# Block 2's projections in 512-wide matmuls, and bias tables copied by another queue

## The chip, the cores and the metric

One NeuronCore of one Trainium2 chip runs the whole program. The time is device microseconds of one execution, from launch to end. The engines are TensorE (PE in the profile, its weight loads PEld), VectorE (DVE), ScalarE (ACT), GpSimd (POOL) and SyncE (SP). They run side by side, each through its own queue of instructions in order, and wait for each other on semaphores.

## What is computed

Two transformer blocks on 256 tokens of width 1024, in float32. Block 1 has a gated convolution and recurrent mixer, cross-attention to a memory, and a mixture of 16 experts whose router picks a group and two experts in it. Block 2 has two layers over the tokens and 256 context tokens. In each layer one projection of the normalised input feeds three kinds of attention and their gates:

```
(na_q, na_k, na_v, cq, ckv, k_rope, dq, dk, dv, z, gm) = split(h @ w_in_l)
q, k = rms_norm(per head) * g ; rotary turn on some
o_na   = neighbourhood attention with a bias from na_rpb (8 heads of 64)
o_mla  = attention with low-rank q and k, v (8 heads of 96, w_uq, w_ukv)
o_diff = softmax(q0 k0) - lam * softmax(q1 k1), times v (4 heads)
y = sum over the three: sigmoid(gm_i) * ((o_i * silu(z_i)) @ w_br_i)
x = x + gate * (y @ w_out)
```

## The kernel before

Every large product is made of three: an operand is split into a rounded high part and the rest (`hi`, `lo`, type fp32r), and hi·hi + hi·lo + lo·hi are summed in PSUM. Weights arrive by SyncE's queue in units of 128 x 1024 numbers (512 KB, `_wdma`, L458), ScalarE makes the high part `wh`, VectorE the low part `wl` (`splitter`), and TensorE reads both. The small tiles all bear the name `t`, PSUM banks the name `p`, so the profile shows them so; nearly every operation is recorded by a helper (L369 matmul, L374 transpose, L382 ScalarE, L392 and its neighbours VectorE), so a group is known by its tiles. Names stand as out<-in, the moving operand first and the stationary one behind it.

There are two kinds of product. In `gemm_w` and `gemm_f` the weights are stationary and the tokens move (`p<-t,wh`). In `gemm_x`, `gemm_m` and `gemm_t` 128 tokens are stationary and the weights move (`p<-wh,t`, `p<-wl,t`). `gemm_t` (L683) serves Block 2: keys, values and queries of the neighbourhood and differential attention (`keys`, `queries`), the keys and values of the low-rank attention (`w_ukv_2` in `mla_half`), and the last projection `w_out_2` (`out`). It goes over 256 columns of weights at a time; a PSUM bank of 512 columns holds both halves (m = 0, 1) of one stream's 256 tokens side by side. A stream is the tokens (0) or the context (1); `both` asks for two.

What follows a product is its evacuation, spawned when its last matmul is out. For keys and queries that is `ev_qk`: ScalarE squares the bank, VectorE reduces it to a sum per head, `rsqrt` takes the root in ten small VectorE instructions (one root for both column halves, by `sums` and `roots`), VectorE multiplies the bank by it into a tile and frees the bank, a rotary turn follows for some, and `heads_T` transposes on TensorE and writes the heads by `put`. Values go through `ev_vals`, low-rank keys through `ev_kv`.

The program is written by a planner inside the kernel. Each piece of work is a generator (a fiber) with a priority and a time; `run` takes the fiber that TensorE, by the planner's own costs, could start first, and every instruction is put into its engine's queue when its fiber runs. PSUM has eight banks (`palloc`): products take at most six at a time, attention's scores and transposes four, its outputs three. A request for several banks waits until all are free. The order in which weight units are loaded is what the pass before asked for: a first pass without an order, then `PASSES` = 2 passes with the order of the one before, and the last is the program that runs.

For the neighbourhood attention, `prepare` (L921) writes for both layers a table of the bias in DRAM (`toep`), by sixteen copies from DRAM to DRAM of 448 rows of 64 numbers, issued on ScalarE's queue at L953; `TOEP` = 3000 ns of the planner's time lie between them. `attend` loads biases from it on GpSimd's queue (L2223). `GR` = 4 says that `out` goes over four column groups together for the first stream.

Of the kernel before, what the change touches and what calls it, by code (L numbers as in the profile page):

```python
# [13 lines left out]
AF = mybir.ActivationFunctionType  # L14
# [40 lines left out]
PASSES = 2  # L55
# [85 lines left out]
class Core:  # L141
# [15 lines left out]
    MEMT, TOEP, CRIT = 40000, 3000, -4  # L157
# [5 lines left out]
    GR, GP = 4, 0.5  # L163
# [519 lines left out]
    def gemm_t(self, name, lead, K, c0, c1, hi, lo, streams, evac, cw=256, base=0, kev=None, group=1):  # L683


        kt = K // 128
        evs = []
        for g in range(c0, c1, group * cw):
            pss = []
            for _ in range(group):  # L690
                ps = yield from self.palloc("pg", len(streams))
                pss.append(ps if len(streams) > 1 else [ps])
            for u in range(0, kt, 4):
                u1 = min(kt, u + 4)
                for i, ps in enumerate(pss):
                    c = g + i * cw
                    w = yield from self.wget(name, lead, u, u1, c, c + cw)
                    for p, s in zip(ps, streams):
                        for m in range(2):
                            o = p[:, m * cw:m * cw + cw]  # L700
                            t0 = T * (1 - s) + m * 128 - base
                            ts = slice(t0, t0 + 128)
                            for k in range(u, u1):
                                if kev:
                                    yield from self.wait(kev[k])
                                self.mm(o, hi.k(k)[:, ts], w.hi[:, k - u], m == 0 and k == 0, False)
                                self.mm(o, hi.k(k)[:, ts], w.lo[:, k - u], False, False)
                                self.mm(o, lo.k(k)[:, ts], w.hi[:, k - u], False, m == 1 and k == kt - 1)
                        if p is not ps[-1]:
                            yield  # L710
                    self.wput(w)
                    if u1 == kt:
# [208 lines left out]
    def prepare(self):  # L921
# [858 lines left out]
    def layer(self, l, hi, lo, C, ready, half=None):  # L1780
# [52 lines left out]
        def heads_T(raw, np_, nb, dst, d0, gain):  # L1833

            for j0 in range(0, nb, 2):
                jn = min(2, nb - j0)
                ps = yield from self.palloc("pa")
                pv = ps.rearrange("p (j t) -> p j t", j=2)
                for j in range(jn):
                    for m in range(2):  # L1840
                        self.tr(pv[:np_, j, m * 128:m * 128 + 128], raw(m, j0 + j))
                yield
                put(dst, slice(d0 + j0, d0 + j0 + jn), np_, slice(0, T), pv[:np_, :jn], gain)
                self.free(ps)
                yield
# [21 lines left out]
        def ev_qk(streams, gcol, dst, tab):  # L1867

            ns = len(streams)
            sh = yield from sums(2, ns * 8)  # L1870

            def evac(i, pss):
                ss = sh["ss"][:, i * ns * 8:(i + 1) * ns * 8].rearrange("p (m h) -> p m h", h=4)
# [9 lines left out]
                rv = r.rearrange("p (m h) -> p m h", h=4)  # L1883
                raws = []
                for a in range(ns):
                    rw = yield from self.alloc("S", [128, 2, 4, 64])
                    self.tt(rw, pv[a], rv[:, 2 * a:2 * a + 2][:, :, :, None].to_broadcast([128, 2, 4, 64]))
                    self.free(pss[a])
                    raws.append(rw)
                drop(sh)  # L1890
                yield
                for a, s in enumerate(streams):
                    rw = raws[a]
                    turn = tab is not None and s == 0
                    if turn:
                        yield from rope(rw, tabs[tab], 4, 64)
                    yield from heads_T(lambda m, j: rw[:, m, 2 * j:2 * j + 2].rearrange("p h d -> p (h d)"), 128, 2,
                                       dst[s], 2 * i, 1.0 if turn else gcol)
# [3 lines left out]
        def ev_vals(streams, v):  # L1902
            def evac(i, pss):
                for a, s in enumerate(streams):
                    self.act(v[s].kk(0, 2)[:, :, i * 256:i * 256 + 256], pss[a].rearrange("p (m c) -> p m c", m=2))
                    self.free(pss[a])
                    yield
            return evac

        def keys(ck, cv, gk, rot, streams):  # L1910
# [4 lines left out]
            ev = yield from ev_qk(streams, self.colv(gk, l), k, gk if rot else None)  # L1915
# [3 lines left out]
            evs += yield from self.gemm_t(W, (l,), D, cv, cv + 512, hi, lo, streams, ev_vals(streams, v))  # L1919
            return k, v, evs  # L1920

        def queries(cq, gq, rot, streams):
# [3 lines left out]
            ev = yield from ev_qk(streams, self.colv(gq, l), q, gq if rot else None)  # L1926
# [71 lines left out]
        def mla_half(i, lt):  # L1998
# [8 lines left out]
            shk = yield from sums(2, 8)  # L2007
            shq = yield from sums(2, 4 * ns)

            def ev_kv(c, pss):  # L2010
                ss = shk["ss"][:, c * 8:c * 8 + 8].rearrange("p (m h) -> p m h", h=2)
                t0 = self.cur.t
                pv = [p.rearrange("p (m h d) -> p m h d", m=2, h=2) for p in pss]
                sq = yield from self.alloc("S", [128, 4, 2, 64])
                for m in range(4):
                    p = pv[m // 2][:, m % 2]
                    r = st[:, 1, m:m + 1]
                    self.act(sq[:, m], p[:, :, 0:64], AF.Square, scale=r, after=t0)
                    self.act(v[1 - m // 2][:, m % 2].rearrange("p (h d) -> p h d", h=4)[:, 2 * c:2 * c + 2], p[:, :, 64:128], scale=r,
                             after=t0)  # L2020
                self.red(ss, sq)
                self.free(sq)
                self.tt(ss, ss, st[:, 2][:, :, None].to_broadcast([128, 4, 2]), OP.add)
                yield
                r = yield from roots(shk, c, 1.0 / 96)
                rv = r.rearrange("p (m h) -> p m h", h=2)
                rr = yield from self.alloc("T", [128, 4, 2])
                self.tt(rr, rv, st[:, 1][:, :, None].to_broadcast([128, 4, 2]))
                raws = []
                for a in range(2):  # L2030
                    rw = yield from self.alloc("S", [128, 2, 2, 96])
                    m2 = slice(2 * a, 2 * a + 2)
                    self.tt(rw[:, :, :, 0:64], pv[a][:, :, :, 0:64], rr[:, m2][:, :, :, None].to_broadcast([128, 2, 2, 64]))
# [706 lines left out]
```

## Time and profile before

| what | us |
|---|---|
| median of three runs | 1623.51 (1622.63 to 1624.02) |
| the profiled execution | 1620.66 |
| its span, first to last instruction | 1618.9 |
| TensorE busy in the span | 1560.7 |
| VectorE busy | 978.6 |
| ScalarE busy | 753.3 |
| GpSimd busy | 41.6 |

Busy is the union of an engine's instructions in the span. Matmuls overlap in the records, so the pace of a run of matmuls is read from their starts. The share of full clock that TensorE was granted stands in the windows as PEclk. In brackets behind a row of a timeline stands how long the engine had idled before it and what ended that; "issue" is idling for which the profile shows no releaser.

### The profile page before, as it was taken

To read this page: it belongs to the slowest core of one execution; us is meant where nothing else is said; L and a number is where in the kernel's file an instruction comes from. 1 tells how busy PE (TensorE), PEld (TensorE's weight loads), DVE (VectorE), ACT (ScalarE), POOL (GpSimd) and SP (SyncE) were. 2 spreads that over 40 slices of the span, in tenths; PEclk is the share of its full clock that TensorE was granted. 3 is DMA by queue.
4 is the path that set the end of the run, shared out by engine and by line. 5 is a ranking of instruction groups with operands and counts; after the bars stand their busy time and mean duration, and the time that the engine had idled before them with its cause. 6 is when DMAs were issued, how large, how long until landed. Compare 5 with 4: busy or idle time off the path is not lost.

```text
span 1618.9 us, 28924 instructions
## 1 busy us (share of the span) xinstructions
PE 1560.7 (96%) x11642; PEld 1319.7 (82%) x11642; DVE 978.6 (60%) x2035; ACT 753.3 (47%) x1357; POOL 41.6 (3%) x75
## 2 busy tenths in 40 slices
PE   6999999799999999999999999999989989999898
PEld 5898899653565558998888777889989989989898
DVE  5877457613232239778855555655866766867765
ACT  4524455333322127757743444553445464645552
POOL 0000000000000001011000000000100100000000
PEclk9999999899999999999999999999999999999999
DMA  9666556869999994665333444424655414333531
GB/s 342 230 215 222 182 182 194 283 249 383 372 381 336 378 377 151 182 175 118 92 110 110 145 133 149 137 74 157 206 156 156 119 53 144 112 102 106 157 110 62
DMA packets 233176, 305.31 MB, mean 189 GB/s; under 512 B 17184, under 2 KB 160288, under 8 KB 233040
## 3 DMA queue, kind: packets, MB, share of 16 engines
q1 hardware_dynamic: 222608, 293.11, 55.9%
q0 software_dynamic: 2576, 7.77, 1.6%
q10 hardware_dynamic: 7856, 2.56, 0.8%
q8 instruction: 93, 1.52, 0.4%
q14 instruction: 43, 0.35, 0.1%
HBM read 302.34 MB, written 2.90 MB: 189 GB/s over the span
## 4 chain that ended last, share of the span: by engine, by line
PE 61%; DVE 4%; ACT 2%; DMA 1%; issue 1%; DVEq 0%; ACTq 0%
PE p L369 56%; PE p L374 4%; ACT t L382 1%; DVE t L392 1%; DVE t L404 1%; DVE wl L392 1%; DMA w<-in_w_in_dram 1%; ACT wh L382 0%; DVE t L397 0%; DVE t L413 0%; DVE t L411 0%; DVE t L399 0%; DVE t L406 0%; DVE X L392 0%; ACT X L382 0%
## 5 line engine op out<-in xcount | busy, mean ns | idle before, releaser
L369 PE MATMUL p<-t,wh 128*128 128x256 f32 (+1 forms) x2640 | 562.6, 310 | 0.6 <-DVE t L392 0.6
L369 PE MATMUL p<-wh,t 128*128 128x256 f32 (+2 forms) x2248 | 466.2, 302 | 7.4 <-DVE t L392 5.7
L392 DVE TENSOR_TENSOR wl<-w,wh 128x1024 fp32r<-128x1024 f32 (+2 forms) x318 | 372.7, 1189 | 161.5 <-ACT wh L382 159.9
L369 PEld LDWEIGHTS p<-t,wh 128*128 128x128 f32 x2640 | 424.8, 190 | 35.0 <-issue 10.5
L369 PE MATMUL p<-t,wl 128*128 128x256 f32 (+1 forms) x1312 | 399.8, 305 | 4.0 <-DVE wl L392 4.0
L382 ACT ACTIVATE t<-p 128x512 f32<-128x512 f32 (+5 forms) x381 | 192.5, 528 | 443.9 <-PE p L369 335.3
L369 PEld LDWEIGHTS p<-wh,t 128*128 128x128 f32 x2248 | 367.0, 193 | 31.3 <-issue 8.8
L382 ACT ACTIVATE wh<-w 128x1024 fp32r<-128x1024 f32 (+2 forms) x318 | 319.4, 1032 | 52.1 <-issue 18.7
L369 PE MATMUL p<-wl,t 128*128 128x256 f32 (+2 forms) x1124 | 335.9, 299 | 0.9 <-DVE wl L392 0.9
L369 PEld LDWEIGHTS p<-t,wl 128*128 128x128 f32 x1312 | 250.1, 191 | 15.6 <-DVE wl L392 4.8
L369 PE MATMUL p<-t,t 128*64 128x128 f32 (+8 forms) x1824 | 220.4, 309 | 2.7 <-ACT t L382 1.6
L369 PEld LDWEIGHTS p<-wl,t 128*128 128x128 f32 x1124 | 216.6, 193 | 6.8 <-DVE wl L392 2.1
L369 PEld LDWEIGHTS p<-t,t 128*64 128x64 f32 (+3 forms) x1824 | 176.5, 171 | 38.7 <-issue 17.3
L369 PE MATMUL p<-w,t 128*64 128x512 f32 x768 | 174.0, 597 | 0.3 <-PEq L1641 0.3
L382 ACT ACTIVATE t<-p,t 128x512 f32<-128x512 f32 (+3 forms) x232 | 120.1, 559 | 115.6 <-PE p L369 75.2
L374 PE MATMUL p<-csts,t 128*128 128x128 f32 (+1 forms) x848 | 120.5, 282 | 24.4 <-ACT t L382 9.0
L374 PEld LDWEIGHTS p<-csts,t 128*128 128x128 f32 (+1 forms) x848 | 98.2, 143 | 41.9 <-issue 16.1
L369 PEld LDWEIGHTS p<-w,t 128*64 128x64 f32 x768 | 52.1, 136 | 95.0 <-issue 87.8
L392 DVE TENSOR_TENSOR t<-t,t 128x512 f32<-128x512 f32 (+9 forms) x254 | 108.8, 461 | 13.3 <-ACT t L382 10.4
L382 ACT ACTIVATE t<-p,cols 128x256 fp32r<-128x256 f32 (+4 forms) x91 | 49.9, 604 | 118.9 <-PE p L374 83.7
L404 DVE SCALAR_TENSOR_TENSOR t<-t,p 128x512 f32<-128x512 f32 x70 | 47.6, 683 | 84.4 <-ACT t L382 45.4
L411 DVE TENSOR_REDUCE t<-p 128x1 f32<-128x512 f32 (+1 forms) x124 | 84.8, 684 | 21.4 <-PE p L369 20.2
(95 smaller groups left out, 678.3 us busy)
## 6 DMA issues: line engine op xcount, KB each, us to landing
w<-in_w_in_dram SPq DMA_DIRECT2D x206, 512.0 KB, 4.3
w<-in_w_gate_dram SPq DMA_DIRECT2D x64, 512.0 KB, 8.6
w<-in_w_up_dram SPq DMA_DIRECT2D x64, 512.0 KB, 10.2
w<-in_w_down_dram SPq DMA_DIRECT2D x64, 512.0 KB, 10.3
w<-in_w_ada_dram SPq DMA_DIRECT2D x48, 512.0 KB, 3.7
w<-in_w_out_dram SPq DMA_DIRECT2D x32, 512.0 KB, 4.6
w<-in_w_br_dram SPq DMA_DIRECT2D x28, 512.0 KB, 3.4
w<-in_w_kv_dram SPq DMA_DIRECT2D x16, 512.0 KB, 4.8
```

The costliest lines, as they stand in the source:

```text
L369: self.nc.tensor.matmul(out, lhsT, rhs, start=start, stop=stop)
L374: self.nc.tensor.transpose(out, in_, self.ident[:k, :k])
L382: self.nc.scalar.activation(out, in_, func, bias=bias, scale=scale, **kw)
L392: self._e(eng, self._n(out), False, after).tensor_tensor(out, a, b, op=op)
L404: e.scalar_tensor_tensor(out, a, s, b, op0=op0, op1=op1)
L411: e.tensor_reduce(out, a, axis=AX, op=op, negate=True)
```

## The change

- `gemm_t` takes 512 columns at a time (units of 2 x 512 rows and columns in place of 4 x 256; 128 tokens now fill a bank of their own), so it asks for two banks for each stream. With `each`, every 128 tokens are evacuated as soon as their last matmul is out; values and `out` use that.
- `ev_qk`, `ev_kv`, `ev_vals`, `out` and `heads_T` follow that layout: one evacuation for 512 columns with its own root, transposes of four blocks of one half of the tokens. The turn is made for each half over 8 heads.
- `GR` is 2 in place of 4 (of twice the width). The output leaves as 128 tokens x 512 columns.
- The sixteen table copies are issued on GpSimd's queue, and `TOEP` is 20000.
- `PASSES` is 4, and the last pass takes, of the orders of the three before it, the one with the earliest planned end.

```diff
-PASSES = 2
+PASSES = 4
-    MEMT, TOEP, CRIT = 40000, 3000, -4
+    MEMT, TOEP, CRIT = 40000, 20000, -4
-    GR, GP = 4, 0.5
+    GR, GP = 2, 0.5
...
-    def gemm_t(self, name, lead, K, c0, c1, hi, lo, streams, evac, cw=256, base=0, kev=None, group=1):
+    def gemm_t(self, name, lead, K, c0, c1, hi, lo, streams, evac, cw=512, base=0, kev=None, group=1, each=False):
         kt = K // 128
+        ku = 1024 // cw
         evs = []
+        tiles = [T * (1 - s) + m * 128 - base for s in streams for m in range(2)]
         for g in range(c0, c1, group * cw):
             pss = []
             for _ in range(group):
-                ps = yield from self.palloc("pg", len(streams))
-                pss.append(ps if len(streams) > 1 else [ps])
-            for u in range(0, kt, 4):
-                u1 = min(kt, u + 4)
+                ps = yield from self.palloc("pg", len(tiles))
+                pss.append(ps)
+            for u in range(0, kt, ku):
+                u1 = min(kt, u + ku)
                 for i, ps in enumerate(pss):
                     c = g + i * cw
                     w = yield from self.wget(name, lead, u, u1, c, c + cw)
...
+                    for a, (p, t0) in enumerate(zip(ps, tiles)):
+                        ts = slice(t0, t0 + 128)
+                        for k in range(u, u1):
+                            if kev:
+                                yield from self.wait(kev[k])
+                            self.mm(p[:, :cw], hi.k(k)[:, ts], w.hi[:, k - u], k == 0, False)
+                            self.mm(p[:, :cw], hi.k(k)[:, ts], w.lo[:, k - u], False, False)
+                            self.mm(p[:, :cw], lo.k(k)[:, ts], w.hi[:, k - u], False, k == kt - 1)
+                        if u1 == kt and each:
+                            evs.append(self.spawn(evac((c - c0) // cw, a, p), prio=self.cur.prio - self.EVAC,
+                                                  name=f"evt {name} {c}"))
+                        if a % 2 and a < len(tiles) - 1:
                             yield
...
-                nc.scalar.dma_start(
+                nc.gpsimd.dma_start(
                     d[:, h].rearrange("c (r k) -> r c k", r=7),
...
+            n = 2 * len(streams)
+
+            def evac(_, pss):
+                ss = yield from self.alloc("T", [128, n, 8])
                 t0 = self.cur.t
-                pv = [p.rearrange("p (m h d) -> p m h d", m=2, h=4) for p in pss]
-                for a in range(ns):
-                    sq = yield from self.alloc("S", [128, 2, 4, 64])
+                pv = [p.rearrange("p (h d) -> p h d", h=8) for p in pss]
+                for a in range(n):
+                    sq = yield from self.alloc("S", [128, 8, 64])
                     self.act(sq, pv[a], AF.Square, after=t0)
-                    self.red(ss[:, 2 * a:2 * a + 2], sq)
+                    self.red(ss[:, a], sq)
                     self.free(sq)
                 yield
-                r = yield from roots(sh, i, 1.0 / 64)
+                r = yield from self.rsqrt(ss.rearrange("p a h -> p (a h)"), 1.0 / 64, n * 8)
...
+                for a in range(n):
+                    rw = yield from self.alloc("S", [128, 8, 64])
+                    self.tt(rw, pv[a], rv[:, a][:, :, None].to_broadcast([128, 8, 64]))
                     self.free(pss[a])
                     raws.append(rw)
...
-            evs += yield from self.gemm_t(W, (l,), D, cv, cv + 512, hi, lo, streams, ev_vals(streams, v))
+            evs += yield from self.gemm_t(W, (l,), D, cv, cv + 512, hi, lo, streams, ev_vals(streams, v), each=True)
...
+            def evac(i, m, ps):
+                c = slice(i * 512, i * 512 + 512)
+                tmp = yield from self.alloc("S", [128, 512])
+                self.tt(tmp, ps, g[:, c])
+                self.free(ps)
+                self.tt(res[m][:, c], tmp, res[m][:, c], OP.add)
                 self.free(tmp)
...
+    if order is None:
+        _passes.clear()
+    elif len(_passes) == PASSES - 1:
+        order = min(_passes, key=lambda x: x[0])[1]
     core = Core(tc.nc, tc, ctx, ins, out, order)
     core.program()
+    if order is not None:
+        _passes.append((max(core.E[e] for e in ("pe", "act", "dve")), order))
```

## Rows read from the trace of the kernel before

**Rows 1.** The page's first part: busy us, share of the span, instructions.

```profile
PE 1560.7 (96%) x11642; PEld 1319.7 (82%) x11642; DVE 978.6 (60%) x2035; ACT 753.3 (47%) x1357; POOL 41.6 (3%) x75
```

**Rows 2.** Groups by form on TensorE: shapes, count | busy us, mean ns | idle before.

```profile
L369 PE MATMUL p<-wh,t 128*128 128x256 f32 x1920 | 362.9, 287 | 6.0 <-DVE t L392 5.7 <-ACT t L382 0.2
...
L369 PE MATMUL p<-wl,t 128*128 128x256 f32 x960 | 273.8, 285 | 0.6 <-DVE wl L392 0.6
```

**Rows 3.** Timeline of TensorE at 1600 us: start us, us, instruction, count.

```profile
1600.11 0.40 PE L369 MATMUL p<-wh,t 128*128 128x256 f32 x2
...
1600.47 0.40 PE L369 MATMUL p<-wh,t 128*128 128x256 f32 x2
```

**Rows 4.** Timeline of TensorE at 146 us, `gemm_x`.

```profile
146.26 0.62 PE L369 MATMUL p<-wh,t 128*128 128x512 f32 x2
...
146.94 0.62 PE L369 MATMUL p<-wh,t 128*128 128x512 f32 x2
```

**Rows 5.** Timeline of all engines, 295 to 307 us; ACTq is ScalarE's queue.

```profile
295.88 0.28 PE L369 MATMUL p<-t,wrl 128*20 128x256 f32 x1
...
296.57 8.57 ACTq L953 DMA_DIRECT2D toep<-in_na_rpb_dram  x3
...
305.19 1.06 ACT L382 ACTIVATE wh<-w 128x1024 fp32r<-128x1024 f32 x1 [10.19 <-issue]
306.16 0.45 ACT L382 ACTIVATE t<-p,cols 20x256 f32<-20x256 f32 x1
...
306.66 0.40 PE L374 MATMUL p<-csts,t 20*128 20x20 f32 x2 [7.62 <-ACT t L382]
```

**Rows 6.** Windows: us, busy us (instructions) by engine, PEclk, DMA share, GB/s.

```profile
230.00:240.00 10.00, 10.00 (x52) 8.51 (x51) 5.38 (x10) 5.91 (x12) 0.00 (x0) 1.00 0.46 138
300.00:310.00 10.00, 3.34 (x14) 3.01 (x15) 3.06 (x6) 2.84 (x4) 0.00 (x0) 0.62 0.91 215
310.00:320.00 10.00, 8.59 (x62) 8.38 (x60) 7.74 (x33) 3.39 (x6) 0.00 (x0) 0.86 0.62 212
350.00:360.00 10.00, 10.00 (x65) 5.93 (x62) 0.65 (x2) 4.86 (x14) 0.00 (x0) 1.00 1.05 387
1135.00:1147.00 12.00, 12.00 (x102) 12.00 (x102) 8.43 (x9) 8.22 (x9) 0.00 (x0) 1.00 1.06 345
```

**Rows 7.** The copies' line: ns min/median/max of an issue, first and last start.

```profile
L953 ACTq DMA_DIRECT2D toep<-in_na_rpb_dram x16: 755/1059/4437, 244.0 to 301.9; - x16
```

**Rows 8.** Waits of SyncE's queue: us in total, times, longest us.

```profile
SPq L458 <- DMA toep<-in_na_rpb_dram: 24.4, 5, 8.1
```

**Rows 9.** Timeline of GpSimd.

```profile
522.83 0.55 POOL L1445 DMA_DIRECT2D t<-in_final_norm_dram  x1 [297.92 <-PE p L369]
...
700.02 2.46 POOL L2223 DMA_DIRECT2D t<-toep  x4 [72.63 <-PE p L369]
709.54 2.38 POOL L2223 DMA_DIRECT2D t<-toep  x4 [7.06 <-DVE wl L392]
```

**Rows 10.** Timeline of VectorE and TensorE, 1308 to 1311 us.

```profile
1308.61 2.48 DVE L392 TENSOR_TENSOR t<-p,t 128x512 f32<-128x512 f32 x4
1309.36 0.55 PE L369 MATMUL p<-wh,t 128*128 128x256 f32 x1 [5.11 <-DVE t L392]
...
1309.92 0.63 PE L369 MATMUL p<-wh,t 128*128 128x256 f32 x2
...
1310.56 0.63 PE L369 MATMUL p<-wh,t 128*128 128x256 f32 x2
```

**Rows 11.** Timeline of VectorE, 706 to 712 us.

```profile
706.88 2.36 DVE L392 TENSOR_TENSOR wl<-w,wh 128x1024 fp32r<-128x1024 f32 x2 [1.78 <-ACT wh L382]
...
710.96 1.22 DVE L392 TENSOR_TENSOR wl<-w,wh 128x1024 fp32r<-128x1024 f32 x1 [0.26 <-ACT wh L382]
```

**Rows 12.** Timeline of TensorE, two waits in Block 2's layer 1.

```profile
1210.82 3.47 PE L374 MATMUL p<-csts,t 128*128 128x128 f32 x16 [5.96 <-DVE t L397]
...
1510.24 1.47 PE L374 MATMUL p<-csts,t 128*128 128x128 f32 x8 [3.57 <-DVE t L392]
```

More of the change, by code (lines that the diff above doesn't have):

```diff
@@ L697, in gemm_t @@
                     w = yield from self.wget(name, lead, u, u1, c, c + cw)
[L698 to L709, printed above, removed]
+                    for a, (p, t0) in enumerate(zip(ps, tiles)):
[10 more added lines that the diff above has]
+                        if a % 2 and a < len(tiles) - 1:
                             yield
                     self.wput(w)
-                    if u1 == kt:
+                    if u1 == kt and not each:
                         evs.append(self.spawn(evac((c - c0) // cw, ps), prio=self.cur.prio - self.EVAC, name=f"evt {name} {c}"))
@@ L1831, in put, with heads_T @@
                 self.stt(dst[1][:np_, js, ts], src, g, hd.bitcast(F32), OP.mult, OP.subtract)
[L1833 to L1845, printed above, removed]
+        def heads_T(raw, np_, m, dst, gain):
+            ps = yield from self.palloc("pa")
+            pw = ps.rearrange("p (j t) -> p j t", j=4)
+            for j in range(4):
+                self.tr(pw[:np_, j], raw(j))
+            yield
+            put(dst, slice(0, 4), np_, slice(m * 128, m * 128 + 128), pw[:np_], gain)
+            self.free(ps)
+            yield
         def sums(n, cols):
@@ L1902, in ev_vals, with evac @@
         def ev_vals(streams, v):
[L1903 to L1907, printed above, removed]
+            def evac(_, a, ps):
+                self.act(v[streams[a // 2]].k(a % 2), ps)
+                self.free(ps)
+                yield
             return evac
@@ L2006, in mla_half, with ev_kv @@
             ns = len(act_)
[L2007 removed]
             shq = yield from sums(2, 4 * ns)
[L2010 to L2011 removed]
+            def ev_kv(_, pss):
+                ss = yield from self.alloc("T", [128, 4, 4])
                 t0 = self.cur.t
[L2013 to L2023, printed above, removed]
+                pv = [p.rearrange("p (h d) -> p h d", h=4) for p in pss]
+                for a in range(2):
+                    sq = yield from self.alloc("S", [128, 2, 4, 64])
+                    for m in range(2):
+                        p, r = pv[2 * a + m], st[:, 1, 2 * a + m:2 * a + m + 1]
+                        self.act(sq[:, m], p[:, :, 0:64], AF.Square, scale=r, after=t0)
+                        self.act(v[both[a]][:, m].rearrange("p (h d) -> p h d", h=4), p[:, :, 64:128], scale=r, after=t0)
+                    self.red(ss[:, 2 * a:2 * a + 2], sq)
+                    self.free(sq)
+                self.tt(ss, ss, st[:, 2][:, :, None].to_broadcast([128, 4, 4]), OP.add)
@@ L2036, in ev_kv @@
                     self.free(pss[a])
                     raws.append(rw)
-                self.free(rr)
-                drop(shk)
+                self.free(rr, ss, r)
                 yield
-                for a, s in enumerate(both):
-                    rw = raws[a]
-                    yield from heads_T(lambda m, j: rw[:, m, j], 96, 2, k[s], 2 * c, self.colv("mla_k_col", 2 * l + s))
+                for a in range(4):
+                    rw, s = raws[a], both[a // 2]
+                    yield from heads_T(lambda j: rw[:, j], 96, a % 2, k[s], self.colv("mla_k_col", 2 * l + s))
```

66 lines of the change are left out of this document (23 added, 43 removed).

## The prediction

> **What bounds the kernel now.** I read the views in this order: the page's busy shares, the groups by form, the timeline of TensorE at both widths, then everything around the longest holes in TensorE. The page says where to look: TensorE is busy 1560.7 of 1618.9 us, VectorE 60% and ScalarE 47% [rows 1]. So 58 us of the span are holes in TensorE, and the other 1560 us are the steps between its matmuls. A change can help in two ways: shorten the steps, or close holes.
>
> The steps have to be read from starts, not from durations, because the durations overlap (two matmuls of 0.28 us make one of 0.40 us). Three matmuls 256 columns wide start over 1600.11 to 1600.47, so one takes 120 ns [rows 3]. Three matmuls 512 wide start over 146.26 to 146.94, so one takes 227 ns [rows 4]. Twice 120 is 240: the same columns in one instruction cost 13 ns less than in two. That is a fixed part of some 13 ns per matmul, and columns that cost 0.418 ns each, (227 - 120)/256. The token-stationary matmuls (weights moving) number 1920 + 960 = 2880 at 256 columns, and both of their counts are exactly what `gemm_t`'s calls add up to; the 512-wide ones of the same kind come from `gemm_x`: 2880 is the number that changes [rows 2].
>
> Of the holes, the longest is at 299 us. The router's logits are finished on TensorE at 295.88 + 0.28 us; ScalarE, which has to bring them out of PSUM, starts that at 306.16. In between its queue stands in three issues of bias-table copies, 8.57 us from 296.57, and ScalarE's own row says it idled 10.19 us for "issue". TensorE's next instruction, which needs the logits, waits 7.62 us [rows 5]. Then it is punished again: in 300 to 310 the granted clock is 0.62 on average and in 310 to 320 0.86, where it is 1.00 in 230 to 240 [rows 6]; TensorE had just idled. An issue that waits for nothing takes 755 ns, but these range up to 4437 ns, and SyncE's weight loads in turn waited 24.4 us in five places for these very copies [rows 7, 8]. So the two queues hold each other up over copies that nobody reads before 700 us, when GpSimd first loads a bias from them [rows 9].
>
> **The change part by part.**
>
> *Width.* It turns 2880 matmuls of 256 columns into 1440 of 512. TensorE gains 1440 x (240 - 227) = **18.7 us**, and the stationary loads beside them halve. Nearly all of it lies where TensorE is the bound. About 288 of the 2880 (the context's differential attention) lie in the expert stage, where the DMA engines are full (share 1.05, 387 GB/s at 350 to 360) [rows 6]; there 144 x 13 = 1.9 us of TensorE may be swallowed. But their weights now come in rows of 2 KB in place of 1 KB. The expert weights already do, at 387/1.05 = 369 GB/s per full share; a stretch of 1 KB rows moves 345/1.06 = 325 [rows 6]. Twelve units of 524288 bytes take 19.4 us at the one and 17.1 at the other, 2.3 us less. So I leave the 18.7 whole; its lower end is 16.
>
> The TensorE page of the Trainium skill (TensorE: Matmul & The Clock Gate, section Back-to-back issue gap) speaks against this part: it gives the isolated gap of a warm matmul as columns/2.4 plus 2.5 ns, a fixed part five times smaller than rows 3 and 4 show. By that rule the width would be worth 1440 x 2.5 = 3.6 us. The trace disagrees at both widths, and I go by the rows.
>
> *Copies.* Sixteen copies leave ScalarE's queue for GpSimd's. The hole of 7.62 us closes, since ScalarE is otherwise free when the logits are done. TensorE then also keeps its clock. At the lower of the two levels (1.2 GHz) three 256-wide matmuls start over 1309.92 to 1310.56, 213 ns each against 120 [rows 10]. The clock's share of 0.62 and 0.86 over two times 10 us is worth about 5 us of full clock in total, half of which fell in the hole; what remains is about 2.5 us. That makes **10.0 us** (7.6 + 2.5, rounded). A cross-check: the logits leave PSUM at 306.16 where 296.2 would do, 9.96 us earlier, and the routing chain behind starts that much sooner. What is late next is that chain itself. Cover for it shrinks only by its own share of narrower steps, half a microsecond. Low end: if ScalarE is late for another reason, 0.
>
> What it costs on GpSimd: its queue is nearly empty there. It issues a DMA at 522.83 after 297.92 us of idling, so the one before ended at 224.9, and the first loads that read the tables start at 700.02, four in 2.46 us [rows 9]. The planner spreads the copies 20 us apart, but GpSimd's queue has nothing in front that holds them, so I expect a burst soon after 225 us. Sixteen issues at about 0.6 us each (2.46/4) are 10 us of an idle queue; an upper bound for 448 short rows each is ScalarE's longest, 4.4 us, 70 us in all, still done by 300. Behind them wait only the final norm's gain at 522.83 and the first bias. DMA share in 230 to 240 is 0.46 [rows 6], so the copies find room there. VectorE's 1024-wide subtraction at 710.96, beside GpSimd's issues of 709.54 to 711.92, took 1.22 us; the two before it, with no issue beside them, took 2.36 together [rows 9, 11]. So I cost the neighbour at nothing. If the copies did spread into the full DMA stage, 16 x 448 rows of 256 bytes, 1.8 MB, at 369 GB/s would be 5 us; that is the upper end.
>
> *PSUM.* `gemm_t` now asks for two banks at once for one stream and four for two streams, and holds them until the sum of squares, root and product are done. Before, half as many were asked at a time. The row that prices this is at 1309: layer 1's differential keys for both streams hold four banks, the values' first matmul needs two and waits 5.11 us until the products free them, four in 2.48 us [rows 10]. Afterwards that place needs all four banks, two products more (1.24 us), and two of the reductions that ran under the second half of the keys now come behind the last matmul (at the products' 0.62 us each, an estimate: 1.24 us): 2.5 us longer. Other gemms run beside attention that TensorE can turn to. I take two such places, **5 us lost**; ends 0 (attention covers it) and the rival below.
>
> *Small things, near zero.* The rotary turns need 8 VectorE instructions per tensor in place of 12 with the same elements; the latent keys' evacuation halves its ScalarE instructions; both engines have slack (60% and 47%). Output rows leave as half the tokens by 512 columns, the same bytes; the last tile's tail is one product and one sum of 512, as long as one of 512 and two of 256. `GR` goes from 4 to 2 with doubled width, so the same four banks.
>
> *Order of weights.* Four passes in place of two, and the best by the planner's own clock. No row shows what that gives. Bounded by the holes that are left: 58 - 7.6 = 50 us, of which a fifth either way is 10. I take 0, and keep -10 to +8.
>
> **Sum.** Span 1618.9 - 18.7 - 10.0 + 5 = 1595.2 us. Around the span lie 1620.66 - 1618.9 = 1.8 us: 1597.0. The median of the runs shown is 2.85 us above the profiled execution: 1599.9, so **1600 us**, 1.4% less.
>
> **Rivals.**
> 1. *Bank starvation, slower.* Seventeen calls of `gemm_t` end in the root-and-product evacuation. If each next one has to wait for a pair of banks as at 1309, one costs 5.1 us plus about 1.5 for the low clock behind it (an estimate: some 16 matmuls at 213 for 120 ns), 6.6. The gain of 28.7 is used up from the fifth place on. With eight: 1624 - 29 + 53 = 1648. For it: TensorE found no cover at 1304 to 1309. Against it: only this one of the seventeen shows such a wait before, though the two halves' banks were already held together for the shared root. Chance 0.07, and 0.03 more that four or five places eat the gain and leave the time as it was.
> 2. *The copies were not the cause.* The router's hole stays, because the chain behind the logits is the bound, or GpSimd's copies block something. Then 1600 + 10 = 1610. Against it: the issue rows stand exactly in the hole. 0.13.
> 3. *Width is worth little.* The fixed part falls away only partly, as when the wider matmul waits for its operands; with 2.5 ns per matmul kept, 3.6 in place of 18.7 us: 1615. That is what the rule of the Trainium skill quoted above would give. Against it: 512-wide steps of 227 ns in the same kernel. 0.04.
> 4. *The new order also closes chain holes.* The waits of 5.96 us at 1210 (norm of layer 1), 3.57 at 1510 (latent queries' root) and 5.11 at 1309 [rows 10, 12] are 14.6 us that another order could cover: 1600 - 15 = 1585. For it: best of three by the planner's estimate. 0.16.
>
> **How the numbers follow.** The forecast has 0.57, its own range 1590 to 1610 (ends of the bank term, 16 to 18.7 for the width, the order's share). The range of 8 in 10 takes in rivals 2 and 4: 1584 to 1614. A difference under 0.2% (3 us) is about what measuring this kernel can't tell from none. Faster: forecast, rivals 2, 3 and 4, 0.90; same 0.03; slower 0.07.
>
> **What would show it.** Right: 1440 token-stationary matmuls of 512 in place of 2880, three of them starting over 0.68 us; TensorE's busy time down by nearly 19 us; no issue on ScalarE's queue between 240 and 310, no TensorE wait of 7 us there, granted clock 1.00 in 300 to 312; the copies in a burst on GpSimd's queue before 300. Wrong: new waits of TensorE on VectorE's products behind keys and queries, with the clock falling after each; VectorE's 1024-wide subtraction longer than 1.22 us while GpSimd issues; the hole before the routing chain as long as before; or a sum of TensorE waits well off 50 us, which would put it on the order.

## The result and the profile after

| | before | after |
|---|---|---|
| median, us | 1623.07 (1619.24 to 1624.02) | 1587.33 (1586.08 to 1589.04) |
| profiled execution, us | 1620.66 | 1586.62 |
| its span, us | 1618.9 | 1584.8 |
| TensorE busy, us | 1560.7 | 1540.4 |
| rest of the span, us | 58.2 | 44.4 |

The ratio is 0.978 (0.9765 to 0.9795): 35.7 us less, where the forecast had 23. The time lies inside the range given (1584 to 1614) and 12.7 us below the value. Of the 34.1 us that the span lost, 20.3 are TensorE's busy time and 13.8 are holes.

The page's first part of after, which answers rows 1:

```profile
PE 1540.4 (97%) x10202; PEld 1234.6 (78%) x10202; DVE 974.0 (61%) x1995; ACT 749.4 (47%) x1321; POOL 56.8 (4%) x91
```

TensorE has 11642 - 10202 = 1440 matmuls fewer, and GpSimd 16 instructions more, the copies. The groups by form of after, which answer rows 2: the 2880 matmuls of 256 columns are gone, and 1216 + 608 = 1824 of 512 stand there, 1440 from `gemm_t` and the 384 that `gemm_x` had before.

```profile
L369 PE MATMUL p<-wh,t 128*128 128x512 f32 x1216 | 395.2, 397 | 2.3 <-DVE t L404 1.9 <-PEq L1644 0.3
...
L369 PE MATMUL p<-wl,t 128*128 128x512 f32 x608 | 239.1, 393 | 3.3 <-DVE wl L392 3.2
```

The place of rows 10, in the timeline of TensorE of after (layer 1, differential keys, then values):

```profile
1263.74 3.84 PE L369 MATMUL p<-t,t 64*128 64x256 f32 x40 [0.38 <-ACT t L382]
1267.50 0.50 PE L369 MATMUL p<-wh,t 128*128 128x512 f32 x1
...
1269.46 0.62 PE L369 MATMUL p<-wh,t 128*128 128x512 f32 x2
1269.91 0.39 PE L369 MATMUL p<-wl,t 128*128 128x512 f32 x1
1270.14 0.39 PE L369 MATMUL p<-wh,t 128*128 128x512 f32 x1
...
1274.83 0.80 PE L369 MATMUL p<-wh,t 128*128 128x512 f32 x1 [1.94 <-DVE t L404]
```

Two things are to be seen. Three wide matmuls start over 1269.46 to 1270.14, 0.68 us, so one takes 227 ns, as rows 4 had it. And the 5.11 us that the values waited for banks are gone: scores and attention's products fill the time in which VectorE works off the keys, and the longest wait left there is 1.94.

The router, in the timeline of all engines of after (answers rows 5):

```profile
293.92 0.28 PE L369 MATMUL p<-t,wrl 128*20 128x256 f32 x1
...
294.24 0.47 ACT L382 ACTIVATE t<-p,cols 20x256 f32<-20x256 f32 x1 [0.43 <-PE p L369]
...
294.76 0.88 PE L374 MATMUL p<-csts,t 20*128 20x20 f32 x6 [0.56 <-ACT t L382]
```

ScalarE fetches the logits as soon as they are out, and the hole of 7.62 us is 0.56. GpSimd's queue in after has the copies:

```profile
221.07 0.57 POOL L1252 DMA_DIRECT2D t<-in_ffn_norm_dram  x1 [139.97 <-DMA w<-in_w_in_dram]
221.63 6.62 POOL L956 DMA_DIRECT2D toep<-in_na_rpb_dram  x8
...
233.20 1.64 POOL L956 DMA_DIRECT2D toep<-in_na_rpb_dram  x2 [0.23 <-DMA toep<-in_na_rpb_dram]
...
520.75 0.59 POOL L1448 DMA_DIRECT2D t<-in_final_norm_dram  x1 [285.91 <-DMA w<-in_w_down_dram]
521.33 1.66 POOL L956 DMA_DIRECT2D toep<-in_na_rpb_dram  x2
```

Fourteen issues in a burst from 221.63, 0.82 us each, where 0.6 was estimated, and two that the planner queued behind the final norm's load, so they wait until 520.75. What the burst does to its neighbours stands in the windows of after (columns as in rows 6), against rows 6:

```profile
230.00:240.00 10.00, 7.73 (x40) 6.06 (x38) 4.80 (x13) 4.67 (x14) 4.11 (x5) 1.00 1.05 287
300.00:310.00 10.00, 9.94 (x42) 7.82 (x41) 7.71 (x31) 6.33 (x10) 0.00 (x0) 0.91 0.40 113
```

At 300 to 310 TensorE is busy 9.94 in place of 3.34 us; its granted clock there is 0.91, behind waits at 290 to 300 of which the longest is 1.87 us (on VectorE's `wl`), so the 1.00 that the prediction gave as a sign was not reached. And 230 to 250, which was full before, now has holes, with the DMA share at 1.05 in its first half. Two of them, 1.24 and 0.42 us at 234 and 235, wait for a norm on VectorE and have nothing to do with the burst (experiment 7, where the copies come later, has them too, with 1.19 and 0.46). The timeline of all engines of after names what the other two wait for:

```profile
239.67 0.34 ACT L382 ACTIVATE wrh<-t 128x160 fp32r<-128x160 f32 x1 [4.61 <-DMA t<-in_wr_dram]
...
240.55 2.05 PE L369 MATMUL p<-t,t 128*128 128x256 f32 x8 [1.16 <-ACT t L382]
...
243.25 0.23 DVE L406 SCALAR_TENSOR_TENSOR t<-t 128x64 f32<-128x64 f32 x1 [2.88 <-DMA t<-in_lrows_dram]
...
244.69 1.56 PE L369 MATMUL p<-t,t 128*128 128x256 f32 x6 [2.10 <-ACT t L382]
```

Two small loads of `prepare`, the router's weights `wr` and the rows `lrows`, are issued on ScalarE's queue at 233.08 and 233.45 us, when the burst on GpSimd's queue is at its end (the last copy is issued at 234.0) and the DMA engines are still busy with it. ScalarE and VectorE wait for them in the middle of their queues, and the evacuations that TensorE needs stand behind.

### The profile page after: what moved, and what is told of

Read it like the earlier page. It is cut to its first block, busy times and chain, and to the rows that moved or that the text cites. A ratio compares the mean times of both kernels' runs of the same rounds, so it can differ in the third digit from the quotient of the medians.

```text
span 1584.8 us, 25949 instructions
## 1 busy us (share of the span) xinstructions
PE 1540.4 (97%) x10202; PEld 1234.6 (78%) x10202; DVE 974.0 (61%) x1995; ACT 749.4 (47%) x1321; POOL 56.8 (4%) x91
## 4 chain that ended last, share of the span: by engine, by line
PE 60%; DVE 4%; ACT 1%; issue 1%; DVEq 0%; ACTq 0%
PE p L369 56%; PE p L374 4%; DVE t L392 1%; ACT t L382 1%; DVE wl L392 1%; DVE t L404 1%; DVE t L411 0%; ACT wh L382 0%; DVE t L413 0%; DVE X L392 0%; DVE p L392 0%; DVE t L397 0%; DVE t L399 0%; DVE t L406 0%; DVE t L420 0%
## 5 line engine op out<-in xcount | busy, mean ns | idle before, releaser
L392 DVE TENSOR_TENSOR wl<-w,wh 128x1024 fp32r<-128x1024 f32 (+3 forms) x314 | 371.4, 1205 | 149.7 <-ACT wh L382 144.0
L369 PE MATMUL p<-wh,t 128*128 128x512 f32 (+1 forms) x1288 | 414.8, 394 | 2.3 <-DVE t L404 1.9
L382 ACT ACTIVATE wh<-w 128x1024 fp32r<-128x1024 f32 (+3 forms) x314 | 316.8, 1042 | 58.5 <-PE p L369 23.4
L369 PEld LDWEIGHTS p<-wh,t 128*128 128x128 f32 x1288 | 242.8, 189 | 59.2 <-issue 6.8
L369 PE MATMUL p<-wl,t 128*128 128x512 f32 (+1 forms) x644 | 251.1, 390 | 3.3 <-DVE wl L392 3.2
L382 ACT ACTIVATE t<-p,t 128x512 f32<-128x512 f32 (+2 forms) x200 | 115.2, 597 | 126.6 <-PE p L369 84.0
L369 PEld LDWEIGHTS p<-wl,t 128*128 128x128 f32 x644 | 121.9, 189 | 27.1 <-DVE wl L392 5.1
L411 DVE TENSOR_REDUCE t<-p 128x1 f32<-128x512 f32 (+1 forms) x124 | 84.7, 683 | 29.4 <-PE p L369 28.2
```

What stands on the lines that cost most here:

```text
L369: self.nc.tensor.matmul(out, lhsT, rhs, start=start, stop=stop)
L382: self.nc.scalar.activation(out, in_, func, bias=bias, scale=scale, **kw)
L392: self._e(eng, self._n(out), False, after).tensor_tensor(out, a, b, op=op)
L411: e.tensor_reduce(out, a, axis=AX, op=op, negate=True)
```

## The experiments

Each is compared with the kernel before, run on the same chip; medians of before were 1624.7 (experiments 1 to 4), 1624.6 (5 to 8) and 1624.0 (9 to 11). Against these, the 1623.07 beside after are 1 to 1.6 us less, and a difference of medians between an experiment and after is uncertain by that much; where it matters, the difference of the ratios is given too, as a share of before. No experiment leaves out work.

| | | median, us | ratio (interval) | span |
|---|---|---|---|---|
| 1 | copies alone | 1623.41 | 0.9999 (0.9985 to 1.0013) | 1623.4 |
| 2 | width alone | 1609.42 | 0.9913 (0.9887 to 0.9939) | 1604.6 |
| 3 | after, two passes | 1608.24 | 0.9907 (0.9881 to 0.9933) | 1605.8 |
| 4 | after, copies on ScalarE | 1594.86 | 0.9816 (0.9794 to 0.9838) | 1592.0 |
| 5 | after, each wide matmul in two | 1601.41 | 0.9851 (0.9826 to 0.9875) | 1600.5 |
| 6 | selection of the order alone | 1625.75 | 1.0009 (0.9993 to 1.0026) | 1629.7 |
| 7 | after, copies held back | 1583.59 | 0.9746 (0.9725 to 0.9767) | 1581.0 |
| 8 | before, copies held back | 1613.76 | 0.9933 (0.9908 to 0.9958) | 1609.3 |
| 9 | 7 with two passes | 1600.77 | 0.9867 (0.9828 to 0.9905) | 1595.8 |
| 10 | 7 with three passes | 1599.29 | 0.9845 (0.9809 to 0.9881) | 1598.5 |
| 11 | 1 with `TOEP` of before | 1622.06 | 0.9982 (0.9961 to 1.0004) | 1622.8 |

**1. The copies alone.** Before, with the part on the copies.

```diff
-    MEMT, TOEP, CRIT = 40000, 3000, -4
+    MEMT, TOEP, CRIT = 40000, 20000, -4
...
-                nc.scalar.dma_start(
+                nc.gpsimd.dma_start(
```

> The kernel before with only the sixteen table copies issued on GpSimd's queue (and TOEP 20000); widths, passes and order of weights are those of before. Theory: the 7.62 us hole of TensorE at 299 us and the low clock behind it go, 10 us: a ratio of 0.9938, about 1613 us. But the burst of copies delays the two small loads on ScalarE's queue, for which the kernel after shows waits of ScalarE of 4.6 us and TensorE holes of 1.2 and 2.1 us near 240 us: if these come here too, 3 us less, about 1616. Rival (the copies were not the cause): same time as before within 3 us. Rival (a larger part of the surplus lies here): 1605 or less.

The router's hole closed, and nothing was won. The timeline of the experiment, all engines:

```profile
244.85 0.34 ACT L382 ACTIVATE wrh<-t 128x160 fp32r<-128x160 f32 x1 [6.35 <-DMA t<-in_wr_dram]
...
245.72 2.82 PE L369 MATMUL p<-t,t 128*128 128x256 f32 x6 [4.46 <-ACT t L382]
...
302.48 0.28 PE L369 MATMUL p<-t,wrl 128*20 128x256 f32 x1
...
302.80 0.47 ACT L382 ACTIVATE t<-p,cols 20x256 f32<-20x256 f32 x1
```

The logits leave PSUM at 302.80, 3.4 us earlier than before (306.16), not 10: TensorE itself finishes them at 302.5 in place of 296, since it has a new hole of 4.46 us that ends at 245.72, and behind it, over 245 to 255, it was granted 0.83 of its clock. The hole has moved forward, from 299 to 241 us. The last 3 us are lost again in the expert stage (first expert matmul 3.0 us earlier than before, last one 0.6 later); whether that is the copy that leaves at 321.69 and the two at 520 or scatter was not separated, but experiment 11 bears on it.

**2. The width alone.** After, with copies and passes as before. Its units differ from those of before, so its order of loads is its own.

```diff
-PASSES = 4
+PASSES = 2
...
-    MEMT, TOEP, CRIT = 40000, 20000, -4
+    MEMT, TOEP, CRIT = 40000, 3000, -4
...
-                nc.gpsimd.dma_start(
+                nc.scalar.dma_start(
```

> The kernel before with only the 512-wide gemm_t, its evacuations and GR 2; copies on ScalarE's queue, two passes, so the order of weights is that of the second ordered pass. Theory as forecast: 18.7 us of TensorE's steps less, 5 us of bank waits more: about 1609, ratio 0.9915. Theory that the surplus lies in the order: the steps are saved but this order has more holes, so 1615 to 1630, and the time comes only with the selected order. Rival (fixed part of 2.5 ns): 1620.

15.3 us less by the medians, 14.3 by the spans. Timeline of ScalarE and of TensorE:

```profile
288.59 11.02 ACTq L956 DMA_DIRECT2D toep<-in_na_rpb_dram  x4
...
303.02 0.81 PE L374 MATMUL p<-csts,t 20*128 20x20 f32 x3 [12.75 <-ACT t L382]
...
1200.94 1.35 PE L374 MATMUL p<-csts,t 128*128 128x128 f32 x4 [5.75 <-DVE t L397]
```

The router's hole is even longer, 12.75 us, since the logits are done at 290.27, less than 2 us into an issue of four copies (288.59 to 299.61); the chain hole of rows 12 is still there (5.75 for 5.96). The wait for banks of rows 10 is 1.96 us. So nothing of the feared loss appears, with two passes as before. TensorE is busy 1543.3 us, 17.4 less than before, and its holes are 3.1 us more.

**3. After with two passes.** The first hunk of experiment 2 alone.

> The kernel after with PASSES 2, that is, the last pass takes the order of the pass before it in place of the best of three; all else as after. If the forecast's sum holds without any selection: 1600. If the order carries the surplus of 12.7 us: 1600 or more, with TensorE's holes 12 us or more above the 39.5 us of the kernel after in the sum of the waits. If the order is worth nothing: 1587 as after.

20.9 us slower than after. In this order the copies went behind the final norm's load, into the full DMA stage. Timelines of GpSimd and TensorE, then a window:

```profile
514.19 0.59 POOL L1448 DMA_DIRECT2D t<-in_final_norm_dram  x1 [288.14 <-DMA w<-in_w_down_dram]
514.77 5.73 POOL L956 DMA_DIRECT2D toep<-in_na_rpb_dram  x7
...
541.24 1.97 PE L369 MATMUL p<-w,t 128*64 128x512 f32 x4 [4.33 <-DMA w<-in_w_down_dram]
...
520.00:540.00 20.00, 15.90 (x63) 6.51 (x61) 3.20 (x3) 3.88 (x5) 5.45 (x7) 1.00 0.80 218
```

The same window of experiment 9 below, which runs the same instructions in the same order and has no copy there:

```profile
520.00:540.00 20.00, 19.66 (x88) 8.58 (x88) 3.95 (x4) 3.86 (x5) 0.00 (x0) 1.00 0.80 294
```

With thirteen short-row copies issued from 514.77 to 528, the same DMA share of 0.80 moves 218 in place of 294 GB/s, and expert weights come late: from the first to the last expert matmul it takes 282.4 us, in experiment 9 it takes 272.2. The chain hole before layer 1 is there as well (5.75 us). So the 20.9 us have two causes, the copies' place and the order; experiment 9 tells them apart.

**4. After with the copies back on ScalarE.** The other two hunks of experiment 2.

> The kernel after with the copies back on ScalarE's queue and TOEP 3000; widths and the selected order as after. Theory: ScalarE is held near the router again, TensorE waits some 7 us there and its clock falls: about 1597, ratio to before 0.984. If the copies' gain were only before's particular order: 1587 as after. If the burst costs 3 us near 240: 1594.

7.5 us slower than after (5.8 by the ratios). TensorE's timeline has the router's hole, and the 7.1 us by which TensorE ends later (1587.1 in place of 1580.0) are there from the expert stage on (last expert matmul 607.8 in place of 600.7):

```profile
303.66 1.23 PE L374 MATMUL p<-csts,t 20*128 20x20 f32 x5 [13.54 <-ACT t L382]
```

Against experiment 2 it differs by the order alone: 14.6 us less by the medians, 12.6 by the spans, and no hole at 1200.

**5. Every wide matmul issued as two halves.** After, same plan, same banks, same units.

```diff
+    def mm2(self, out, lhsT, rhs, start, stop):
...
+        h = n // 2
+        self.nc.tensor.matmul(out[:, :h], lhsT, rhs[:, :h], start=start, stop=False)
+        self.nc.tensor.matmul(out[:, h:], lhsT, rhs[:, h:], start=False, stop=stop)
...
-                            self.mm(p[:, :cw], hi.k(k)[:, ts], w.hi[:, k - u], k == 0, False)
+                            self.mm2(p[:, :cw], hi.k(k)[:, ts], w.hi[:, k - u], k == 0, False)
```

(and so for the other two products)

> The kernel after with every 512-wide matmul of gemm_t issued as two of 256 into the halves of the same bank; the plan is charged as for one, so the order of all else, the units, banks and evacuations stay those of after. Theory (a fixed part of 13 ns per matmul): 1440 more steps of 120 in place of 227 for two, 18.7 us, some of it hidden in the full DMA stage: 1604 to 1606, ratio to before 0.988 to 0.990. Rival (fixed part of 2.5 ns): 1591. Rival (stationary loads, twice as many, are a bound of their own): over 1606.

14.1 us slower than after by the medians, 15.7 by the spans, 11.5 by the ratios. The page's first part, and one group by form of TensorE:

```profile
PE 1557.4 (97%) x11642; PEld 1315.8 (82%) x11642; DVE 973.9 (61%) x1995; ACT 749.3 (47%) x1321; POOL 57.0 (4%) x91
...
L375 PE MATMUL p<-wh,t 128*128 128x256 f32 x960 | 258.0, 288 | 2.2 <-DVE t L411 1.8 <-PEq L1651 0.3
```

TensorE is busy 17.0 us longer: 1440 steps saved are worth 11.8 ns each, where the starts gave 13. This is the part's price by itself, with banks, queues and order unchanged. Every matmul here brings a stationary load of its own, 11642 of each in this run and 10202 of each in after, so the 11.8 ns belong to a matmul with its load; which of the two costs them no run tells.

**6. The selection alone.** Before with four passes and the best of three orders.

```diff
-PASSES = 2
+PASSES = 4
...
+    elif len(_passes) == PASSES - 1:
+        order = min(_passes, key=lambda x: x[0])[1]
```

> The kernel before with only PASSES 4 and the choice of the best of the three orders. Theory that the selection is worth something only against the bad second ordered pass of the wide kernel: same as before within 3 us. Rival (selection by itself finds an order that covers the chain holes): 1611 as the 12.7 us between the wide kernels with copies on ScalarE's queue.

No difference. The order that it took is another one than that of before, but it has the same three holes of rows 10 and 12 (5.10, 5.97 and 3.56 us). The selection is worth something only where one of its orders is better.

**7. The copies held back.** After, with one column of the tile that `lrows` has filled overwritten by GpSimd ahead of the copies, so that they stand behind VectorE's reading of it, and `TOEP` as before, so that they stay together.

```diff
-    MEMT, TOEP, CRIT = 40000, 20000, -4
+    MEMT, TOEP, CRIT = 40000, 3000, -4
...
+        nc.gpsimd.memset(lr[:, 0, 0, 0:1], 0.0)
```

> The kernel after with the copies held back on GpSimd's queue until VectorE has read the small load they delayed (a one-column memset into that tile ahead of the first copy) and TOEP 3000, so that all sixteen stand ahead of the final norm's load; the order of weights is that of after. Theory (the copies cost what they delay): the TensorE holes of 1.16 and 2.10 us at 240 to 245 go and no copy lies in the full DMA stage at 521: 3 to 5 us less than after, 1583, ratio 0.9755. Rival (the holes at 240 come from the new order, not from the copies): 1587.

The fastest of all, 3.7 us below after (5.5 by the ratios). GpSimd's timeline, all sixteen behind the memset:

```profile
237.06 0.10 POOL L940 MEMSET t<- 128x1 f32 x1 [156.59 <-PE p L369]
237.62 1.74 POOL L957 DMA_DIRECT2D toep<-in_na_rpb_dram  x2 [0.46 <-issue]
...
249.22 4.30 POOL L957 DMA_DIRECT2D toep<-in_na_rpb_dram  x5 [0.16 <-issue]
```

The DMA view (last number: us from issue to landing) of the two small loads, with the copies held back and then in after:

```profile
t<-in_lrows_dram ACTq DMA_DIRECT2D x1, 256.0 KB, 3.8
t<-in_wr_dram ACTq DMA_DIRECT2D x1, 80.0 KB, 3.2
```

```profile
t<-in_lrows_dram ACTq DMA_DIRECT2D x1, 256.0 KB, 9.8
t<-in_wr_dram ACTq DMA_DIRECT2D x1, 80.0 KB, 6.6
```

Beside the burst both take more than twice as long, and without it the holes at 240 and 245 are gone.

**8. The same on before.** Copies on GpSimd, held back; width and order of before.

```diff
+        nc.gpsimd.memset(lr[:, 0, 0, 0:1], 0.0)
...
-                nc.scalar.dma_start(
+                nc.gpsimd.dma_start(
```

> The kernel before with only the copies on GpSimd's queue, held back in the same way and with TOEP 3000. Theory (the copies' gain of 10 us was eaten by the hole of 4.5 us at 245 and by what they disturb in the expert stage): 1616 to 1618, ratio 0.996. Rival (the expert stage's end is set by its weight stream, so nothing that comes before it is worth anything in this order): 1623, ratio 1.000, with its first expert matmul 6 us or more earlier and its last one where it was.

10.8 us less than before (7 to 15 by the interval). The forecast's 10.0 for the copies is right for copies that delay no small load; they do run beside weight loads, with a DMA share of 1.08 at 250 to 260, and TensorE is busy throughout those 10 us.

**9 and 10. Experiment 7 with two and with three passes.** The first hunk of experiment 2, with 2 or 3, on 7.

> The kernel with the copies held back (e7) but PASSES 2, the order of the second ordered pass. It tells the order from the copies' place, since no copy can lie in the full DMA stage here. Theory (the order is worth what it was worth with copies on ScalarE's queue, 12.7 us of profile): 1596, with TensorE's hole of 5.75 us before the norm of layer 1 back and the 4.33 us hole of e3 at 541 gone. Rival (most of the 20 us between e3 and after was the copies' place): 1588 or less.

> As e9 with PASSES 3 and no choice, so the last pass takes the order of the second ordered pass, and a third order of the same work runs. Theory (an order is worth what holes it leaves near the chain of layer 1's norm, and orders differ by some 10 us): between 1584 and 1600, its distance from e7 the difference of TensorE's holes and low clock. Rival (only the two-pass order is bad): 1584.

17.2 and 15.7 us slower than 7 by the medians, 14.8 and 17.5 by the spans. With the copies out of the question that is the order's worth here. Experiments 9 and 10 run the second and the third of the three orders that the selection chooses from. After and experiment 7 have neither (their weight loads come in another order from the third on), so the selection took the first, and the further passes brought nothing. A window around the start of layer 1, of experiment 9 and then of 7:

```profile
1090.00:1240.00 150.00, 144.22 (x780) 124.93 (x779) 113.59 (x182) 74.00 (x97) 10.45 (x20) 0.98 0.57 176
```

```profile
1090.00:1240.00 150.00, 149.41 (x824) 129.91 (x823) 120.56 (x189) 77.28 (x100) 12.20 (x20) 1.00 0.60 186
```

The same 150 us hold 44 matmuls more and 5 us of holes less, at full clock. What happens there is seen on VectorE. X is the residual that `out` adds to, L406 the sum of squares of the norm of layer 1, L397 its scaling, which TensorE's transposes need. Timelines of VectorE and TensorE in experiment 9:

```profile
1164.79 0.69 DVE L392 TENSOR_TENSOR X<-t,X 128x512 f32<-128x512 f32 x1
...
1173.70 0.69 DVE L413 TENSOR_REDUCE t<-t 128x8 f32<-128x512 f32 x1 [2.54 <-ACT t L382]
...
1186.93 0.75 DVE L404 SCALAR_TENSOR_TENSOR t<-p,cols,t 128x512 fp32r<-128x512 f32 x1 [1.01 <-ACT t L382]
1187.59 1.22 DVE L406 SCALAR_TENSOR_TENSOR t<-X 128x1024 f32<-128x1024 f32 x1
...
1191.10 0.75 DVE L397 TENSOR_SCALAR t<-X,t 128x1024 f32<-128x1024 f32 x1
...
1191.91 3.92 PE L374 MATMUL p<-csts,t 128*128 128x128 f32 x16 [5.75 <-DVE t L397]
```

X is complete at 1165.5, and the sum of squares starts at 1187.59, 22 us later, though VectorE idled meanwhile (2.54 us at 1173.70): it stands in the queue behind the evacuation of keys of 8 heads, which the reductions to 128x8 show. When the norm comes, that product, its only cover, is done. In experiment 7:

```profile
1162.68 0.69 DVE L392 TENSOR_TENSOR X<-t,X 128x512 f32<-128x512 f32 x1
1163.41 1.23 DVE L406 SCALAR_TENSOR_TENSOR t<-X 128x1024 f32<-128x1024 f32 x1
```

There the norm follows its input at once, the keys' product covers it, and the transposes at 1173.44 wait for nothing. They take 1.91 us; behind the hole of experiment 9, where the granted clock over 1190 to 1200 is 0.70, they take 3.92. After and experiment 4, the same order, start the sum within 0.04 us of X; experiments 2, 3, 9 and 10 all start it 22 us late. In before it is the last columns of `out` that come late (X at 1205.62, 28 us after the columns before), and nothing is left to cover the norm. The order that the selection took is one in which `out` is early and the norm is queued ahead of that product. What in the list of loads makes the planner do so was not isolated. Nor is this place all: the hole and the slow transposes are 7.8 of the 14.8 us of span between experiments 9 and 7. A longer wait at the latent queries' transposes is 1.8 (4.96 in place of 3.19), 1.9 are there by the last expert matmul, and the rest has not been traced.

**11. Experiment 1 without the spread.** `TOEP` back to 3000: one copy leaves early, at 84.7, fifteen in the burst, and none behind the final norm.

> The kernel before with the copies on GpSimd's queue and TOEP 3000 without holding them back: the burst of e1, but none left behind the final norm's load. Theory (both places cost: the hole at 245 some 6 us with its low clock, the stragglers some 4): about 1619, ratio 0.9965. Rival (the delayed small loads are all of it): 1623. Rival (the stragglers are all of it): 1614 as e8.

1.9 us below before, and the interval takes in no difference: the burst beside the small loads is by itself enough to lose most of what experiment 8 wins. What the stragglers cost in experiment 1 is not separated by it. The first expert matmul comes 5.5 us later than there (337.5 for 332.0), behind a longer hole, but from the first to the last one it takes 274.8 us in place of 279.0 (before: 275.3), so in these two traces the stragglers may be worth some 4 us. TensorE's timeline has the hole again:

```profile
246.80 1.65 PE L369 MATMUL p<-t,t 128*128 128x256 f32 x3 [5.50 <-ACT t L382]
```

## Why the prediction was right, and where its steps failed

The direction and the range held. The value was 12.7 us too high, and its terms fail in both directions. That the range held is owed to rival 4, which it took in with a chance of 0.16; the forecast's own range, 1590 to 1610, missed.

| term of the sum, us | forecast | measured |
|---|---|---|
| width, steps alone | -18.7 | -14.1 (experiment 5; -15.7 by the spans, -11.5 by the ratios) |
| waits for PSUM banks | +5 | -3.2 at the place priced (5.11 to 1.96) |
| copies | -10.0 | 0 (experiment 1), -7.5 (4 to after), -10.8 (8), -11.3 (4 to 7) |
| order of weights | 0 | -14.6 (2 to 4), -17.2 (9 to 7) |

*Width.* The mechanism was right: 13 ns from the starts [rows 3, 4] against 11.8 measured; and the 17.0 of busy time became 15.7 of span, since TensorE's holes shrank by the rest. Busy time and span lie about where the lower end of 16 was put, the medians below it. Rival 3 falls: the fixed part is real and nearly all of it was saved. The rule of the Trainium skill weighed there (TensorE: Matmul & The Clock Gate, section Back-to-back issue gap), 2.5 ns for each isolated matmul, would have given 3.6 us, an estimate; experiment 5 took back 14.1. The measurement decides: not so on these matmuls, each with its own stationary load.

*Banks.* This term was wrong. I priced two places at 2.5 us from the one place that waited before [rows 10], and took the wait for one that the banks' number makes longer. No wait there is longer than 1.96 us in the two-pass order or 1.94 in after, because scores and products of attention stood ready at that point. Width alone, banks included, gave 15.3 us in experiment 2. That is about what the steps are worth, but not by them alone: the router's hole grew by 5.1 us there, and the values' wait shrank by 3.2. Rival 1 falls with it. A wait of TensorE says what other work its queue held at that time as much as what it waits for.

*Copies.* The diagnosis was right: ScalarE's issues were the hole, and it closed. The step that failed is "the copies find room there", read from a DMA share of 0.46 before [rows 6], and "Behind them wait only the final norm's gain at 522.83 and the first bias". I had looked for who waits on GpSimd's queue and not for who shares the DMA engines at that moment on another queue. The burst takes the share to 1.05 (1.10 in experiment 1), the two small loads of `prepare` take 6.6 and 9.8 us in place of 3.2 and 3.8, and ScalarE idles 4.6 us in after and 6.4 in experiment 1 for the first of them. Rival 2 had the right effect at the wrong place, "GpSimd's copies block something". With the selected order the loss is 3.7 us, which experiment 7 wins back; with the order of before it was all of the 10. That VectorE runs its subtraction as fast beside GpSimd's issues was right: in experiment 8 the 1024-wide ones beside the copies took 1.22 us each, and its VectorE is busy 978.7 us against 978.6 before, with the same 2035 instructions.

*Order.* The term that I had set at 0 is as large as the width. Rival 4, with 0.16, is nearest to what happened: of the three holes it named [rows 10, 12], 5.96 at layer 1's norm and 5.11 at the values are covered in after. For the 3.57 at the latent queries' root, after has one of 3.21 at transposes close by. Its sum, 14.6 us, is also what experiments 2 and 4 differ by, but that is chance, since the account is another: 5.11 went in every wide order, and the lower clock behind the hole at 1200 came on top (over 1090 to 1240 the granted clock is 1.00 in place of 0.98). My -10 for the upper bound of the order was also too small. What I missed: a pass of the planner writes all queues anew, so its order can win or lose a whole chain hole, here 7.8 us with the clock behind it, and more in other places. And "best of three" was no gain on top of the passes: it kept the first order, where two or three passes would have ended on worse ones. Selection on the kernel before, by contrast, was worth nothing (experiment 6).

Together: 15.3 for the width with its banks, 14.6 for the order and 7.5 for the copies are 37.4 us. These steps lead from before over 2 and 4 to after, so their sum is the whole difference by construction and no check of the split; that after against its own before gave 35.7 only says that the medians of before differ, 1624.7 and 1623.1. The forecast's gain was a third too small, and its split was wrong.

## What to carry to other kernels

A transfer that is moved to an idle queue keeps its load on the DMA engines: look for the small loads that other queues have in flight at the new time, and for the engines that stand in order behind them; holding the burst back by one dependency turned 0 into 10.8 us here. Where a planner writes the queues, test its order apart from the edit that comes with it, with the same edit under two and four passes. A hole in a chain is to be read backwards on the engine that feeds it: if its input was ready long before, the order of its queue is at fault and not the work.

## What the runs showed of the hardware that I had not expected

- A GpSimd issue of one copy (448 rows of 256 bytes) takes 0.82 to 1.03 us, little more than ScalarE's shortest (755 ns), and never the 4.4 us that ScalarE took. In experiment 2, four of them held ScalarE for 11.02 us.
- Thirteen such copies move 1.5 MB, but at the time of the expert weights the traffic over 20 us was 218 GB/s with them and 294 without (experiments 3 and 9), at the same DMA share of 0.80, and the expert stage took 10.2 us longer.
- A load of 80 KB beside the burst took 6.6 and 7.4 us (after, experiment 1) in place of 3.2 and 4.0 (experiments 7, 8).
